# Hybrid decoder layer on one core: attention's output weights in two parts, and the order of the head groups in the first token tile

## The chip, the cores and the metric

The kernel runs on one NeuronCore of a Trainium2 chip (trn2). The metric is the device time of one launch in microseconds (us). The kernel before took 1487.29 us, the median of three runs between 1485.58 and 1488.57 us.

## The reference

One decoder layer over 2048 tokens of width 1024, all in float32. The normed tokens go through one input projection whose columns belong to three groups of heads; each group gives 512 columns, the three are set side by side, and one output projection brings them back to width 1024.

```
proj = rms_norm(x, g_pre) @ w_in
y_rg = rg_lru(conv(rg_x)) * silu(rg_g)                    # group 0: recurrence
y_da = rms_norm(diff_attention(q, k, v)) * silu(da_g)     # group 1: causal differential attention
y_xa = mem_cross_attention(xa_q, km, vm) * silu(xa_g)     # group 2: 256 memory tokens
y = concatenate([y_rg, y_da, y_xa]) @ w_out               # w_out is 1536 x 1024
out = x + rms_norm(y, g_post)
```

## The kernel before, in words

**Numbers in two parts.** Every float32 operand of a large product is split into a high part (a cast on ACT, L237) and a low part (raw minus high, on POOL or DVE, L238; `split_weight`). A product is then three matmuls (`mm3`, L240 to L243): high by high, low by high, high by low. In the output projection the token side is the stationary operand, so the first two matmuls read the high part of the weights and the third the low part.

**Stages.** `project` (L800) runs twice, first for the tokens 0 to 1023, then for 1024 to 2047; each time it walks through 16 pairs of column blocks, and a pair has four units (two token chunks by two halves) of 24 matmuls each. A unit ends in an eviction; for the last pair of the second run, a query and key pair, that is `ev_qk` (L425 to L441), which writes a tile `qkhl` and stores it to DRAM a little later. Attention runs as generators beside the projection: `pump` puts their matmuls between those of the projection when the modelled time `now` says that they are due. The first half of the attention's list of jobs (all heads, tokens 0 to 1023) precedes the second half.

**The output projection** (from L937) goes through 16 token tiles of 128 rows. A tile has two halves of 512 output columns and three head groups; a half and group take four blocks of 128 rows of the weights, 12 matmuls, into one of two PSUM tiles (`psM`, which the projection's units used before). The weights of a group are four blocks of 128x1024 (512 KB), loaded into a raw tile `woraw` and split in two halves of 512 columns, the first half's low part on POOL, the second's on DVE (L919 to L924). The split tokens of a tile and group (`y_granule`, L904) come through a raw tile of 256 KB, `yraw`, and the low part is made on POOL. Group 0's weights and the first granule are loaded inside the last pair, in `last_pair` (L927), which is called ahead of its third unit; the rest follows after the projection. In the first tile (token tile 0) a group is used for both halves before the next group; from tile 1 on all groups of one half come first. When a group's second half is done, the next tile's granule of that group is loaded.

**Buffers.** Groups 0 and 2 have their weights in the large pool (`wout` in the profile). Group 1's are named `wo`: blocks 0 to 2 take the six slots of `pw`, which the input weights (`wp`) held before, and block 3 two slots of `p4`. `p4` has seven slots of 4 KB per partition, and `qkhl`, `woraw`, the granules `yg`, block 3 of `wo`, and in the tiles `res` and `xres` all share them.

**Order.** TensorE's order is the order of the code (manual schedule). The other engines' orders, SP's queue of DMA issues among them, are made ahead of time by a list scheduler: by priority, which falls in the order of the code (some evictions are raised), as far as a cost model thinks operands and slots are ready. All loads and stores here are issued from SP's queue in that order, and one that waits for a slot holds up those behind it.

Of the kernel before, what the change touches and what calls it, by code (L numbers as in the profile page):

```python
# [10 lines left out]
F32R = mybir.dt.float32r  # L11
# [4 lines left out]
D = 1024  # L16
# [41 lines left out]
def hybrid_layer(  # L58
# [19 lines left out]
    pw = ctx.enter_context(tc.tile_pool(name="pw", bufs=6))  # L78
    p4 = ctx.enter_context(tc.tile_pool(name="p4", bufs=7))
# [9 lines left out]
    def f4(name, shape=(128, 1024), dt=F32, pool=p4):  # L89
        return pool.tile(list(shape), dt, tag="f4", name=name)  # L90

    def f2(name, shape=(128, 516), dt=F32, pool=p2):
        return pool.tile(list(shape), dt, tag="f2", name=name)

    def bigt(name, shape, dt=F32R):
        return big.tile(list(shape), dt, tag="big", name=name)

    def ps_m(name, shape=(128, 512)):
        return psM.tile(list(shape), F32, tag="M", name=name)
# [115 lines left out]
    def pump():  # L215
        busy = True
        while busy:
            busy = False
            for st in list(streams):
                if st[0] <= now[0]:  # L220
                    d = next(st[1], None)
                    if d is None:
                        streams.remove(st)
                    else:
                        st[0] = now[0] + d
                    busy = True
# [9 lines left out]
    def split_weight(raw, hi, lo, eng=nc.gpsimd):  # L236
        nc.scalar.copy(hi, raw)  # L237
        eng.tensor_sub(lo, raw, asf(hi))  # L238

    def mm3(o, wh, wl, xh, xl, first, last):  # L240
        mm(o, wh, xh, first, False)
        mm(o, wl, xh, False, False)
        mm(o, wh, xl, False, last)  # L243

    def rsqrt_mean(r, ss, n, eng=nc.gpsimd):

        v = tiny.tile(list(r.shape), F32, tag="rsv", name="rsv")
        t = tiny.tile(list(r.shape), F32, tag="rst", name="rst")
        eng.tensor_scalar(v, ss, 1.0 / n, EPS, op0=ALU.mult, op1=ALU.add)
        nc.scalar.activation(r, v, AF.Ln)  # L250
        nc.scalar.activation(r, r, AF.Exp, scale=-0.5)
        eng.tensor_mul(t, r, r)
        eng.tensor_mul(t, t, v)
        eng.tensor_scalar(t, t, -0.5, 1.5, op0=ALU.mult, op1=ALU.add)
        eng.tensor_mul(r, r, t)
# [346 lines left out]
    normed = set()  # L602
# [299 lines left out]
    wout, grans = {}, {}  # L902

    def y_granule(tt, grp):  # L904
        g = f4("yg", (128, 2, 4, 128), F32R)
        raw = praw.tile([128, 512], F32, tag="raw", name="yraw")
        nc.sync.dma_start(raw, YD[grp][tt // 4][tt % 4])
        split_weight(raw, g[:, 0].rearrange("p a b -> p (a b)"), g[:, 1].rearrange("p a b -> p (a b)"))
        return g


    def load_wout(grp):

        if grp == 1:
            t = [[f4("wo", (128, D), F32R, pw if kb < 3 else p4) for kb in range(4)] for _ in range(2)]
        else:
            bt = [bigt("wout", (128, 4, D)) for _ in range(2)]
            t = [[b[:, kb, :] for kb in range(4)] for b in bt]
        for kb in range(4):  # L919
            raw = f4("woraw")  # L920
            nc.sync.dma_start(raw, w_out[4 * grp + kb])
            for j in range(2):
                cs = slice(j * 512, (j + 1) * 512)
                split_weight(raw[:, cs], t[0][kb][:, cs], t[1][kb][:, cs], nc.vector if j else nc.gpsimd)  # L924
        wout[grp] = t

    def last_pair():  # L927
        grans[0, 0] = y_granule(0, 0)
        load_wout(0)

    project((2, 3), 80, ORDER_B, {(0, 0): start_b, (15, 2): last_pair})


    def y_ready(tt, grp):
        return grp != 1 or all((h, tt // 2) in normed for h in range(4))

    state["kind"] = "out"  # L937
    grans[0, 2] = y_granule(0, 2)
    load_wout(2)
    if y_ready(0, 1):  # L940
        grans[0, 1] = y_granule(0, 1)
    load_wout(1)
    gp = [f2("gp", (128, 512)) for _ in range(2)]
    for j in range(2):
        nc.sync.dma_start(gp[j], g_post[j * 512:(j + 1) * 512].unsqueeze(0).to_broadcast([128, 512]))

    GRP = (0, 2, 1)

    def get_y(tt, grp):
        if (tt, grp) not in grans:  # L950
            drain(lambda: y_ready(tt, grp))
            grans[tt, grp] = y_granule(tt, grp)
        return grans[tt, grp]

    for tt in range(NT):
        res = f4("res")
        ss = tiny.tile([128, 2], F32, tag="oss", name="oss")
        os = [None, None]

        order = [(half, grp) for half in range(2) for grp in GRP] if tt else \  # L960
                [(half, grp) for grp in GRP for half in range(2)]
        for half, grp in order:
            cs = slice(half * 512, half * 512 + 512)
            g, wt = get_y(tt, grp), wout[grp]
            if os[half] is None:
                os[half] = ps_m("po")
            o = os[half]
            for kb in range(4):
                mm3(o, g[:, 0, kb, :], g[:, 1, kb, :], wt[0][kb][:, cs], wt[1][kb][:, cs],
                    grp == GRP[0] and kb == 0, grp == GRP[2] and kb == 3)  # L970
                pump()
            if half == 1:
                del grans[tt, grp]
                if tt + 1 < NT and y_ready(tt + 1, grp):
                    grans[tt + 1, grp] = y_granule(tt + 1, grp)
            if grp == GRP[2]:
                junk = f2("junk", (128, 512))
                nc.scalar.activation(junk, o, AF.Square, accum_out=ss[:, half:half + 1])
                nc.vector.tensor_mul(res[:, cs], o, gp[half])
        r = tiny.tile([128, 1], F32, tag="r3", name="r3")  # L980
        xt = f4("xres")
        nc.sync.dma_start(xt, x[tt * 128:(tt + 1) * 128, :])
        nc.vector.tensor_add(ss[:, 0:1], ss[:, 0:1], ss[:, 1:2])
        rsqrt_mean(r, ss[:, 0:1], D, nc.vector)
        for j in range(2):
            cs = slice(j * 512, (j + 1) * 512)
            nc.vector.scalar_tensor_tensor(res[:, cs], res[:, cs], r, xt[:, cs], op0=ALU.mult, op1=ALU.add)
            if tt == NT - 1:
                nc.sync.dma_start(out[tt * 128:(tt + 1) * 128, cs], res[:, cs])
        if tt < NT - 1:  # L990
            nc.sync.dma_start(out[tt * 128:(tt + 1) * 128, :], res)
# [58 lines left out]
```

## Time and profile before

| | us |
|---|---|
| runs of the kernel before, median (lowest, highest) | 1487.29 (1485.58, 1488.57) |
| the profiled execution | 1490.95 |
| its span in the trace | 1489.10 |
| its mean granted TensorE clock | 0.986 of full speed |

The profiled execution lies 3.66 us above the median, and 1.85 us of it lie outside the span. PE is the matmul engine, PEld its weight loads, DVE VectorE, ACT ScalarE, POOL GpSimd, SPq SyncE's queue of DMA issues. A row of a timeline gives the start, the time from the first start to the last end, engine, line, operation, the tiles and the count of like instructions that were merged; in brackets stands the idle time of the engine before it and what ended it. Matmuls overlap: one is busy for some 0.39 us, and with 512 columns at full clock the next starts 0.23 us after it.

### The profile page before, as it was taken

Reading aid. Unit: us, or ns where it says so; the run is one execution under the profiler, and the core shown is the slowest. Engines: PE = TensorE matmul, PEld = TensorE weight load, DVE = VectorE, ACT = ScalarE, POOL = GpSimd, SP = SyncE. Lnnn points to the kernel's source line nnn. Section 1 sums busy time; section 2 is a strip of 40 time slices with the busy share of each in tenths; the row PEclk is TensorE's granted clock in tenths of the full one; section 3 lists DMA queues with packets and bytes.
Section 4 is the critical chain, followed back from the end, with each engine's and each line's share of the span. In section 5 each row is a group of like instructions: output and inputs, shape, how many; then the busy total and the mean of one; then the engine's idle time right before and its main releaser. Section 6 shows DMA issues by size and latency. Waiting matters only on the chain.

```text
span 1489.1 us, 21951 instructions
## 1 busy us (share of the span) xinstructions
PE 1422.1 (95%) x7568; PEld 1208.6 (81%) x7568; DVE 918.4 (62%) x1862; ACT 811.5 (54%) x1972; POOL 563.8 (38%) x634
## 2 busy tenths in 40 slices
PE   5999999999998899899998999999999999999997
PEld 4789889888886678787786898888877888888886
DVE  6332565677545776757648576767778777777222
ACT  6343545666458674755556555666566545554221
POOL 2231433443446543535425343423346433334221
PEclk9999999999999899999999999999999999999999
DMA  6666666342322146244222543221375234322231
GB/s 218 162 214 219 177 172 206 99 132 82 106 68 64 50 128 187 72 151 123 84 68 71 163 141 128 68 85 40 116 237 174 86 133 151 103 96 76 99 123 70
DMA packets 138655, 184.05 MB, mean 124 GB/s; under 512 B 11440, under 2 KB 81200, under 8 KB 138544
## 3 DMA queue, kind: packets, MB, share of 16 engines
q1 hardware_dynamic: 138400, 182.64, 39.6%
q8 instruction: 59, 0.97, 0.3%
q14 instruction: 52, 0.43, 0.1%
q10 hardware_dynamic: 144, 0.01, 0.0%
HBM read 125.99 MB, written 56.62 MB: 123 GB/s over the span
## 4 chain that ended last, share of the span: by engine, by line
PE 74%; DVE 8%; ACT 6%; POOL 5%; issue 4%; DMA 2%; SPq 0%; DVEq 0%; POOLq 0%; ACTq 0%
PE ip L197 35%; PE po L197 17%; PE s L197 7%; PE o L197 6%; PE pt L201 4%; DVE e L719 2%; PE xas L197 2%; PE kv L197 1%; POOL e L718 1%; PE xao L197 1%; POOL wp L238 1%; DMA wraw<-in_w_in_dram 1%; PE rgo L197 1%; DVE xc L553 1%; ACT e L695 1%
## 5 line engine op out<-in xcount | busy, mean ns | idle before, releaser
L197 PE MATMUL ip<-hnT,wp 128*128 128x512 f32 x2688 | 676.8, 397 | 4.9 <-DVE rgg L563 4.9
L197 PEld LDWEIGHTS ip<-hnT,wp 128*128 128x128 f32 x2688 | 499.0, 190 | 105.8 <-DVE rgg L563 6.1
L695 ACT ACTIVATE e<-s,nm 128x512 f32<-128x512 f32 (+3 forms) x320 | 200.0, 625 | 233.4 <-DVE nm L693 216.3
L238 POOL TENSOR_TENSOR wp<-wraw,wp 128x512 fp32r<-128x512 f32 x133 | 182.2, 1380 | 201.8 <-ACT wp L237 192.8
L693 DVE TENSOR_REDUCE nm<-s 128x1 f32<-128x512 f32 (+3 forms) x320 | 193.2, 605 | 32.4 <-PE s L197 27.7
L197 PE MATMUL po<-wout,yg 128*128 128x512 f32 x768 | 193.5, 393 | 4.2 <-POOL wout L238 1.9
L718 POOL TENSOR_SCALAR e<-e,f 128x512 f32<-128x512 f32 (+3 forms) x160 | 120.3, 767 | 171.1 <-DVE f L714 93.5
L197 PE MATMUL s<-kv,q 128*128 128x512 f32 (+3 forms) x640 | 182.8, 367 | 1.0 <-ACT e L695 0.9
L197 PEld LDWEIGHTS po<-wout,yg 128*128 128x128 f32 x768 | 141.3, 188 | 34.3 <-POOL wout L238 3.3
L719 DVE SCALAR_TENSOR_TENSOR e<-e,f 128x512 f32<-128x512 f32 (+3 forms) x160 | 142.7, 919 | 28.5 <-POOL e L718 28.3
L197 PE MATMUL o<-pthl,kv 128*128 128x256 f32 (+1 forms) x864 | 136.3, 293 | 2.0 <-DVE pthl L760 2.0
L760 DVE TENSOR_TENSOR pthl<-pt,pthl 128x512 fp32r<-128x512 f32 (+1 forms) x144 | 94.6, 657 | 70.4 <-ACT pthl L759 70.0
L197 PEld LDWEIGHTS s<-kv,q 128*128 128x128 f32 x640 | 114.6, 189 | 21.8 <-ACT e L695 1.3
L197 PEld LDWEIGHTS o<-pthl,kv 128*128 128x128 f32 x864 | 116.1, 192 | 5.6 <-DVE pthl L760 2.8
L238 POOL TENSOR_TENSOR yg<-yraw,yg 128x512 fp32r<-128x512 f32 x48 | 64.2, 1341 | 133.1 <-ACT yg L237 122.0
L237 ACT CAST wp<-wraw 128x512 fp32r<-128x512 f32 x144 | 88.2, 618 | 43.9 <-PE ip L197 22.1
L759 ACT CAST pthl<-pt 128x512 fp32r<-128x512 f32 (+1 forms) x144 | 80.8, 561 | 53.3 <-PE pt L201 52.7
L197 PE MATMUL ip<-wp,hnT 128*128 128x256 f32 x768 | 99.4, 284 | 0.0
L197 PE MATMUL po<-wo,yg 128*128 128x512 f32 x384 | 97.3, 392 | 0.0
L197 PEld LDWEIGHTS ip<-wp,hnT 128*128 128x128 f32 x768 | 96.2, 192 | 1.2
L201 PE MATMUL pt<-ident,e 128*128 128x128 f32 x544 | 84.4, 276 | 5.6 <-DVE pthl L760 5.6
L201 PEld LDWEIGHTS pt<-ident,e 128*128 128x128 f32 x544 | 67.9, 142 | 20.8 <-DVE pthl L760 6.0
(183 smaller groups left out, 1731.2 us busy)
## 6 DMA issues: line engine op xcount, KB each, us to landing
wraw<-in_w_in_dram SPq DMA_DIRECT2D x128, 256.0 KB, 2.7
q<-QD SPq DMA_DIRECT2D x128, 128.0 KB, 3.3
kv<-KD SPq DMA_DIRECT2D x24, 512.0 KB, 5.7
kv<-VD SPq DMA_DIRECT2D x24, 512.0 KB, 5.0
yraw<-YD SPq DMA_DIRECT2D x48, 256.0 KB, 2.7
QD<-qkhl SPq DMA_DIRECT2D x32, 256.0 KB, 3.3
KD<-qkhl SPq DMA_DIRECT2D x32, 256.0 KB, 3.7
VD<-vhl SPq DMA_DIRECT2D x32, 256.0 KB, 2.8
```

Of the source, the lines that this page charges most:

```text
L197: nc.tensor.matmul(o, w, xx, start=start, stop=stop)
L201: nc.tensor.transpose(o, i, ident)
L237: nc.scalar.copy(hi, raw)
L238: eng.tensor_sub(lo, raw, asf(hi))
L553: nc.vector.scalar_tensor_tensor(xc[:, 0:CH], xr[:, k:k + CH], vec2[:, cw + k:cw + k + 1], xc[:, 0:CH], op0=ALU.mult, op1=ALU.add)
L693: nc.vector.tensor_reduce(out=nm[:, c, kc:kc + 1], in_=s[:, 0:w], op=ALU.max, axis=AX.X, negate=True)
L695: nc.scalar.activation(e[kc, c][:, 0:w], s[:, 0:w], AF.Exp, bias=nm[:, c, kc:kc + 1], accum_out=l[:, c, kc:kc + 1])
L718: nc.gpsimd.tensor_scalar(e2, e2, f[:, 1, kc:kc + 1], 1.0, op0=ALU.mult, op1=ALU.mult)
L719: nc.vector.scalar_tensor_tensor(e1, e1, f[:, 0, kc:kc + 1], e2, op0=ALU.mult, op1=ALU.add)
L759: nc.scalar.copy(hi[:, 0:n], t[:, 0:n])
L760: nc.vector.tensor_sub(lo[:, 0:n], t[:, 0:n], asf(hi[:, 0:n]))
```

## The change

`load_wout` takes a list of blocks, so that a group can be loaded in two calls. `last_pair` now also loads the first tile's granule of group 1 (where its results are ready) and blocks 0 and 1 of group 1's weights; blocks 2 and 3 are loaded right after the projection, ahead of group 2's granule and weights. Block 1 instead of block 3 takes the two slots of `p4`. The first token tile uses the groups in the order 0, 1, 2; all later tiles keep 0, 2, 1.

```
-    def load_wout(grp):
-        if grp == 1:
-            t = [[f4("wo", (128, D), F32R, pw if kb < 3 else p4) for kb in range(4)] for _ in range(2)]
-        else:
-            bt = [bigt("wout", (128, 4, D)) for _ in range(2)]
-            t = [[b[:, kb, :] for kb in range(4)] for b in bt]
-        for kb in range(4):
+    def load_wout(grp, kbs=range(4)):
+        t = wout.setdefault(grp, [[None] * 4 for _ in range(2)])
+        if grp != 1:
+            for i in range(2):
+                b = bigt("wout", (128, 4, D))
+                t[i][:] = [b[:, kb, :] for kb in range(4)]
+        for kb in kbs:
+            if grp == 1:
+                for i in range(2):
+                    t[i][kb] = f4("wo", (128, D), F32R, p4 if kb == 1 else pw)
             raw = f4("woraw")
             nc.sync.dma_start(raw, w_out[4 * grp + kb])
             for j in range(2):
                 cs = slice(j * 512, (j + 1) * 512)
                 split_weight(raw[:, cs], t[0][kb][:, cs], t[1][kb][:, cs], nc.vector if j else nc.gpsimd)
-        wout[grp] = t
+
+    def y_ready(tt, grp):
+        return grp != 1 or all((h, tt // 2) in normed for h in range(4))
 
     def last_pair():
         grans[0, 0] = y_granule(0, 0)
         load_wout(0)
+        if y_ready(0, 1):
+            grans[0, 1] = y_granule(0, 1)
+        load_wout(1, (0, 1))
 
     state["kind"] = "out"
+    load_wout(1, (2, 3))
     grans[0, 2] = y_granule(0, 2)
     load_wout(2)
-    if y_ready(0, 1):
-        grans[0, 1] = y_granule(0, 1)
-    load_wout(1)
...
-    GRP = (0, 2, 1)
...
+        GRP = (0, 2, 1) if tt else (0, 1, 2)
         order = [(half, grp) for half in range(2) for grp in GRP] if tt else \
                 [(half, grp) for grp in GRP for half in range(2)]
```

## Rows read from the trace of the kernel before

**Rows 1.** The page's part 1, engines: busy us (share), instructions.

```profile
PE 1422.1 (95%) x7568; PEld 1208.6 (81%) x7568; DVE 918.4 (62%) x1862; ACT 811.5 (54%) x1972; POOL 563.8 (38%) x634
```

**Rows 2.** Busy time by stretch: stretch, length, engines' busy us (count), PE clock, DMA share, GB/s.

```profile
1100.00:1150.00 50.00, 45.07 (x214) 36.30 (x214) 40.69 (x77) 30.65 (x77) 31.04 (x29) 0.97 0.66 221
```

**Rows 3.** Groups of PE from 1141 to 1482 us: busy, mean ns, idle before.

```profile
L197 PE MATMUL po<-wout,yg 128*128 128x512 f32 x720 | 179.3, 392 | 1.1 <-DVE res L979 1.1
```

**Rows 4.** PE's timeline, first token tile and the start of the second.

```profile
1109.73 1.55 PE L197 MATMUL po<-wout,yg 128*128 128x512 f32 x6
...
1112.03 1.55 PE L197 MATMUL po<-wout,yg 128*128 128x512 f32 x6
1114.80 0.73 PE L197 MATMUL po<-wout,yg 128*128 128x512 f32 x2 [1.22 <-ACT wout L237]
1116.16 0.60 PE L197 MATMUL po<-wout,yg 128*128 128x512 f32 x1 [0.63 <-POOL wout L238]
...
1120.62 0.65 PE L197 MATMUL po<-wout,yg 128*128 128x512 f32 x2
1121.89 0.98 PE L197 MATMUL po<-wout,yg 128*128 128x512 f32 x3 [0.62 <-POOL wout L238]
1123.57 0.50 PE L197 MATMUL po<-wout,yg 128*128 128x512 f32 x1 [0.70 <-POOL wout L238]
...
1130.39 0.85 PE L197 MATMUL po<-wo,yg 128*128 128x512 f32 x3
...
1136.01 1.58 PE L197 MATMUL po<-wo,yg 128*128 128x512 f32 x6
...
1141.64 2.34 PE L197 MATMUL po<-wout,yg 128*128 128x512 f32 x9 [1.05 <-DVE res L979]
```

**Rows 5.** Busy time in the four microseconds after that stall; the clock stands eighth.

```profile
1116.00:1117.00 1.00, 0.84 (x3) 0.73 (x4) 0.65 (x1) 0.31 (x1) 1.00 (x2) 0.71 0.69 274
1117.00:1118.00 1.00, 1.00 (x7) 0.90 (x5) 0.53 (x2) 0.00 (x0) 1.00 (x2) 0.50 0.45 74
1118.00:1119.00 1.00, 1.00 (x7) 1.00 (x6) 0.42 (x2) 0.71 (x2) 1.00 (x1) 0.50 0.75 283
1119.00:1120.00 1.00, 1.00 (x5) 0.89 (x5) 0.60 (x1) 1.00 (x4) 0.03 (x1) 0.59 0.99 356
```

**Rows 6.** SP's timeline of DMA issues: the loads of weights behind the last pair.

```profile
1106.54 1.86 SPq L921 DMA_DIRECT2D woraw<-in_w_out_dram x3
1112.08 4.98 SPq L921 DMA_DIRECT2D woraw<-in_w_out_dram x2
```

**Rows 7.** SP's waits from 1087 to 1141.7 us: total, times, longest.

```profile
SPq L440 <- ACT qkhl L428: 6.7, 1, 6.7
SPq L921 <- DMA QD<-qkhl: 3.6, 1, 3.6
```

**Rows 8.** Busy time in the last pair's last ten microseconds.

```profile
1096.00:1100.00 4.00, 4.00 (x24) 3.47 (x23) 3.96 (x7) 3.59 (x8) 3.32 (x3) 1.00 0.49 187
1100.00:1105.80 5.80, 5.80 (x31) 4.87 (x31) 4.45 (x12) 1.99 (x7) 3.72 (x6) 1.00 0.72 186
```

**Rows 9.** The tile woraw: time from issue to landing.

```profile
DMA to landing us min/median/max: 3.5/5.6/8.8
```

**Rows 10.** The tile wo: ns min/median/max of each split instruction.

```profile
L237 ACT CAST wo<-woraw x8: 607/620/626, 1124.0 to 1132.9; 128x512 fp32r<-128x512 f32 x8
L238 POOL TENSOR_TENSOR wo<-woraw,wo x4: 1297/1455/1699, 1124.7 to 1134.4; 128x512 fp32r<-128x512 f32 x4
L238 DVE TENSOR_TENSOR wo<-woraw,wo x4: 681/687/812, 1126.4 to 1136.0; 128x512 fp32r<-128x512 f32 x4
```

**Rows 11.** The tile wout: the same subtraction on DVE.

```profile
L238 DVE TENSOR_TENSOR wout<-woraw,wout x8: 678/1300/1356, 1095.6 to 1124.2; 128x512 fp32r<-128x512 f32 x8
```

**Rows 12.** POOL's timeline: the third granule of tile 1.

```profile
1141.44 1.29 POOL L238 TENSOR_TENSOR yg<-yraw,yg 128x512 fp32r<-128x512 f32 x1
```

**Rows 13.** ACT's timeline: the last pair's last eviction.

```profile
1107.83 0.57 ACT L431 CAST qkhl<-ip 128x512 fp32r<-128x512 f32 x1
```

More of the change, by code (lines that the diff above doesn't have):

```diff
@@ L929, in last_pair @@
         load_wout(0)
+        if y_ready(0, 1):
+            grans[0, 1] = y_granule(0, 1)
+        load_wout(1, (0, 1))
     project((2, 3), 80, ORDER_B, {(0, 0): start_b, (15, 2): last_pair})
-    def y_ready(tt, grp):
-        return grp != 1 or all((h, tt // 2) in normed for h in range(4))
     state["kind"] = "out"
+    load_wout(1, (2, 3))
     grans[0, 2] = y_granule(0, 2)
     load_wout(2)
-    if y_ready(0, 1):
-        grans[0, 1] = y_granule(0, 1)
-    load_wout(1)
     gp = [f2("gp", (128, 512)) for _ in range(2)]
```

## The prediction

> **What bounds the kernel now.** I read the page's engine shares first: PE is busy 95% of the span, so time is saved only where PE stands still or runs slowly [rows 1]. The stretches by time come next: from 1100 to 1150 us PE is busy 45.07 of 50 us, the loosest place near the change [rows 2]. Behind it there is nothing to win: from 1141 to 1482 us the output projection's matmuls wait 1.1 us in all [rows 3], so what the first token tile gains or loses arrives whole at the end of the kernel.
>
> PE's own timeline then shows where the idle time lies [rows 4]. Group 0 of tile 0 runs without a gap until about 1113.6. Group 2 is next, and its matmuls stand still four times, each time for its weights `wout`: 1.22 us for a cast, then 0.63, 0.62 and 0.70 us for POOL's low parts, 3.17 us in all. Group 1, the third, starts at 1130.39 and no longer waits for weights. One more wait, 1.05 us at 1141.64, is for DVE to free a PSUM tile. The last view is the clock: in the four microseconds behind the first gap it stands at 0.71, 0.50, 0.50 and 0.59 of full speed, so for a while PE has its lower level, 1.2 instead of 2.4 GHz, right after it was idle [rows 5]. The lost parts add up to 0.29 + 0.50 + 0.50 + 0.41 = 1.70 us. Late weights therefore cost 3.17 + 1.70 = 4.87 us.
>
> Why they are late is in SP's queue: three blocks of group 2 leave at 1106.54, the fourth and the next one only at 1112.08 [rows 6], after a wait of 3.6 us for the store of the last query tile `qkhl`, which held a slot of `p4` [rows 7]. So slots of `p4` already set the pace.
>
> **The change part by part.** *Number of instructions.* None is added or removed: the same 12 blocks and granules are loaded and split, the same matmuls run, in the same places between attention's matmuls, since the first tile has 24 matmuls per group in any order. Only the tiles they read differ.
>
> *Two blocks and one granule move into the last pair.* That is 2 x 512 KB and 256 KB of transfer, five casts on ACT (5 x 0.62 = 3.1 us), three low parts on POOL (two of 1.46, one of 1.29: 4.2 us) and two on DVE. DMA has room: it is 0.49 and 0.72 busy in the two stretches there. ACT has room too (1.99 of 5.80 us from 1100). POOL is busy 3.32 of 4.00 and then 3.72 of 5.80 us, DVE 3.96 of 4.00 and then 4.45 of 5.80 us, a total of 1.39 us free [rows 8]. A low part on DVE takes 0.68 us where it runs alone [rows 10], but its median for `wout` is 1.30 us [rows 11], so two cost 1.4 to 2.6 us. DVE then falls behind by 0 to 1.2 us; attention's three score tiles in PSUM cover that, and I take 0. If the cover is gone, up to 1.2 us appear on PE.
>
> What speaks against the change here is a rule of the Trainium skill, "SBUF — State Buffer", on the shared pair of ports: GpSimd and a DVE operation with two SBUF inputs exclude each other, whichever starts first holds the pair for its whole instruction. The 0.68 against 1.30 us agree with that. By it, the added POOL work of 4.2 us can hold DVE up as well; that is rival D below.
>
> *Two blocks and group 2 stay behind it.* Without idle time and at full clock, the needs of tile 0 move up. By the rows, the second group reaches its third block at 1120.62 - 1.22 - 0.63 - 1.70 = 1117.1, its fourth at about 1118.0 to 1118.7; the third group starts at 1130.39 - 4.87 = 1125.5 and reaches its fourth block at 1136.01 - 4.87 = 1131.1 [rows 4]. Blocks 2 and 3 of group 1 stand in SP's queue where blocks 0 and 1 of group 2 stood. But `p4` is tighter: block 1 of group 1 (two slots) and the granule of group 1 are held from the last pair on, and with group 0's granule and the two `qkhl` tiles that is six of seven. So I let block 2 leave at 1106.54 and block 3 only with the freed slot, at 1112.08 [rows 6]. One turn of a slot is a landing of 3.5 us at best, 5.6 at the median [rows 9], two casts of 0.62 and a low part of 1.46 on POOL [rows 10]: 6.2 to 8.3 us. I take 7.0, nearer the short end, because 1 MB has left this stretch. Block 3 is ready at 1119.1, against 1118.0 to 1118.7: 0.8 us of wait (0 with 6.2 us, 2.3 with 8.3). Group 2's fourth block, third in that slot, is ready at 1112.08 + 3 x 7.0 = 1133.1 if two slots turn, against 1131.1 + 0.8 = 1131.9: 1.2 us late (0 with 6.2, 3.6 with 8.3); if the last `qkhl` store frees a third slot, it isn't late at all. I take 0.5. What remains is 1.3 us, with ends of 0 and 5.9.
>
> *Queues.* A waiting weight load holds up the key store, attention's query loads and tile 1's granules behind it on SP, as the 4.98 us at 1112.08 do now. Six blocks instead of eight stand there now, so these should leave no later; I take 0.
>
> *Tile 1's granules.* They are now asked for in the order 0, 1, 2 but used as 0, 2, 1. The third finishes on POOL at 1141.44 + 1.29 = 1142.7 [rows 12]. In the new order tile 1 wants it after 12 matmuls and some attention, about 3.6 us after its start, which moves from 1141.64 to about 1138.1: at 1141.7. Had POOL's order stayed, that would be 1.0 us late; POOL has lost three low parts ahead of it, so I take 0 and keep 1.0.
>
> *Sum.* -4.87 + 1.3 = -3.6 us on the profiled execution's 1490.95. That one lies 3.66 us above the median, and the difference counts from the median: 1487.29 - 3.6 = **1483.7 us**. About 0.2%, 3 us, is what a measurement of this kernel can tell from no change, so the forecast lies just beyond it.
>
> **The rivals.** *A, part of it comes back:* the turns take nearer 8 us, some 3.4 us of wait remain in groups 1 and 2, and the time is 1487.29 - 4.87 + 3.4 = 1485.8. For it: the longest landing of 8.8 us [rows 9]. Against: these were in the fullest stretch.
>
> *B, the loads don't leave earlier:* SP stands 6.7 us in the last pair, waiting for the third unit's eviction (L440) [rows 7]. If the two blocks are queued behind that, they leave with the others near 1106, and nothing changes: 1487.3. Against: they come before that store in the code, and group 0's raw tiles become free about then.
>
> *C, slower, a slot for the last eviction:* the last unit's `qkhl` needs a slot of `p4` at 1107.83 [rows 13], and its PSUM tile is wanted again by the second half of group 0 at 1109.73 [rows 4]. If the scheduler gives that slot to a weight block, the eviction waits until 1112.08, plus 0.57 for the cast and 0.68 for the low part: 1113.3, so PE stands 3.6 us, and the clock can drop once more (1.7 us). The next slot is then group 0's granule's, free at 1113.6 + 3.6 = 1117.2, so that block 3 is ready at 1124.2 against 1118 + 5.3 = 1123.3, and group 2's last at 1117.2 + 3 x 7.0 = 1138.2 against 1131.1 + 5.3 + 0.9 = 1137.3: 1.8 us more; with turns of 8.3 us it is 5.8. The change is then -4.87 + 5.3 + 1.8 = +2.2 up to +6.2 us; the middle is +4.2, 1491.5 us. It decides as soon as that cast starts later than about 1108.5. For it: six of seven slots are held. Against: evictions have a raised priority, and the low parts of the moved blocks have freed their raw tiles by then.
>
> *D, DVE becomes the bound in the last pair:* two low parts of 1.30 us and 4.2 us of POOL time that hold it up, less the 1.39 us free, would be 5.4 us at worst; if half of that passes attention's cover, 2.7 us, the time is 1483.7 + 2.7 = 1486.4. Against: most of DVE's work there reads scores from PSUM.
>
> **How the numbers follow.** Forecast 0.45, A 0.18, B 0.11, D 0.07, C 0.19. The forecast is faster by over 0.2%; A, B, D and a tenth of C (0.02) are within: 0.38; slower by over 0.2% is the rest of C, 0.17. The range begins at 1481.5: all 4.87 us gone and the 1.05 us of rows 4 as well give 1481.4. It ends at 1489.8, which holds A, B, D and the mild form of C, and leaves out its harder half. The forecast's own range is 1482.0 to 1484.3.
>
> **What would show it.** Right: in the new trace SP issues two `woraw` loads before the last unit ends, PE has under 1.5 us of idle time on `wo` and `wout` in tile 0, the clock stays at full speed there, and tile 1 starts 3 to 4 us earlier measured from the last `ip` matmul. Wrong in part: two low parts of `wo` on DVE before 1105 with PE idle on `s`, or an idle PE ahead of the second weight granule `yg` of tile 1. The forecast falls if the last `qkhl` cast is late with PE idle at group 0's second half, or if the weights of group 2 are now what tile 0 waits for.

## The result, and the profile after

The change made the kernel slower: 1494.81 us median (1493.01 to 1495.87) against 1486.43 us for the kernel before on the same chip, a ratio of 1.0053 with a 95% interval of 1.0036 to 1.0070. The forecast was 1483.7 us, and the result lies above the whole range. The profiled execution has a span of 1493.7 us at a mean granted clock of 0.983.

Upstream of the last pair, where neither the change nor most experiments touch anything, the profiles differ by several us, since the clock falls to its lower level there in three to seven places, with 8.5 to 17.1 us lost. So the stretch of the change is measured by itself: **L** is the time from the end of the last `ip` matmul to tile 1's first `po` matmul. Before, the last `ip` matmuls end at 1104.41 + 1.55 = 1105.96 and tile 1 starts at 1141.64 [rows 4], so L is 35.68 us. In PE's timeline after:

```profile
1101.48 1.55 PE L197 MATMUL ip<-hnT,wp 128*128 128x512 f32 x6
1106.43 1.65 PE L197 MATMUL po<-wout,yg 128*128 128x512 f32 x3 [3.40 <-DVE qkhl L429]
...
1119.50 0.74 PE L197 MATMUL po<-wo,yg 128*128 128x512 f32 x2 [0.52 <-ACT wo L237]
1121.01 0.97 PE L197 MATMUL po<-wo,yg 128*128 128x512 f32 x3 [0.77 <-POOL wo L238]
1122.77 0.50 PE L197 MATMUL po<-wo,yg 128*128 128x512 f32 x1 [0.79 <-POOL wo L238]
...
1135.82 0.73 PE L197 MATMUL po<-wout,yg 128*128 128x512 f32 x2 [1.65 <-ACT wout L237]
1137.17 0.80 PE L197 MATMUL po<-wout,yg 128*128 128x512 f32 x1 [0.62 <-POOL wout L238]
...
1146.03 1.32 PE L197 MATMUL po<-wout,yg 128*128 128x512 f32 x5
```

The last `ip` matmuls end at 1103.03 and tile 1 starts at 1146.03: L is 43.00 us, **7.3 us more**, which agrees with the whole cost of the change (the medians differ by 8.4 us, with 5.4 to 10.4 by the interval). Against rows 4 there is a new wait of 3.40 us ahead of group 0, which belongs to no weight but to the third unit's eviction (L429). Group 1, now second, waits 0.52 + 0.77 + 0.79 = 2.08 us and group 2 1.65 + 0.62 = 2.27 us, where group 2 as second waited 3.17 us before. The 1.05 us for `res` are gone. The clock falls three times instead of once; the stretches by time (stretch, length, busy time of PE, PEld, DVE, ACT, POOL, then clock, DMA share, GB/s), with rows 5 as their counterpart:

```profile
1106.40:1109.80 3.40, 3.37 (x8) 2.70 (x9) 2.81 (x6) 0.11 (x1) 2.24 (x3) 0.53 0.63 125
1123.40:1126.80 3.40, 3.40 (x14) 3.07 (x14) 1.91 (x6) 0.59 (x1) 1.92 (x3) 0.52 0.79 242
1136.90:1143.80 6.90, 6.63 (x19) 5.48 (x20) 3.27 (x5) 4.26 (x11) 5.71 (x7) 0.51 0.51 172
```

That loses 3.40 x 0.47 + 3.40 x 0.48 + 6.90 x 0.49 = 6.6 us. Idle time and lost clock are now 7.75 + 6.6 = 14.4 us, against 3.17 + 1.05 + 1.70 and 0.70 on attention's `pthl`, 6.6 us, before: 7.7 us more, which covers the 7.3. Of these, 3.40 + 1.6 = 5.0 us go with the new wait. The other idle time of PE is even less than before (4.35 against 4.92 us), so the rest is lost clock. From tile 1 on nothing differs: PE is busy 339.92 of 341 us after (from 1146) and 339.88 before (from 1141).

**Why the eviction is late.** The third unit's matmuls end about 1096.0 (its fourth unit is the last 24 `ip` matmuls: 6 from 1101.48, 12 from 1098.27 and the last 6 of 9 from 1095.27). ACT's timeline after:

```profile
1100.14 0.47 ACT L695 ACTIVATE e<-s,nm 128x256 f32<-128x256 f32 x1
1100.51 0.19 ACT L695 ACTIVATION_READ_ACCUMULATOR e<-s,nm 128x1 f32 x1
1100.60 1.13 ACT L237 CAST wo<-woraw 128x512 fp32r<-128x512 f32 x2
1101.63 0.21 ACT L709 ACTIVATE f<-f 128x6 f32<-128x6 f32 x1
1101.74 1.13 ACT L237 CAST wo<-woraw 128x512 fp32r<-128x512 f32 x2
1102.77 0.59 ACT L428 ACTIVATE qkhl<-ip 128x512 fp32r<-128x512 f32 x1
```

and DVE's, which makes the eviction's second part:

```profile
1101.77 1.36 DVE L238 TENSOR_TENSOR wo<-woraw,wo 128x512 fp32r<-128x512 f32 x1 [1.95 <-ACT wo L237]
1103.05 1.22 DVE L710 TENSOR_TENSOR l<-l,f 128x6 f32<-128x6 f32 x1
1104.19 0.68 DVE L693 TENSOR_REDUCE nm<-s 128x1 f32<-128x512 f32 x1
1104.80 0.14 DVE L711 TENSOR_REDUCE r<-l 128x2 f32<-128x6 f32 x1
1104.97 0.17 DVE L712 RECIPROCAL r<-r 128x2 f32<-128x2 f32 x1
1105.08 0.69 DVE L238 TENSOR_TENSOR wo<-woraw,wo 128x512 fp32r<-128x512 f32 x1
1105.69 0.68 DVE L429 SCALAR_TENSOR_TENSOR qkhl<-ip,qkhl 128x512 fp32r<-128x512 f32 x1
```

In ACT's timeline of the kernel before, the same cast stands right at the end of its matmuls:

```profile
1099.09 0.60 ACT L428 ACTIVATE qkhl<-ip 128x512 fp32r<-128x512 f32 x1
```

Now it starts 6.8 us after them. It stands in ACT's order behind the four casts of the moved blocks, and its second part behind their two low parts on DVE; until it is done at 1106.37, group 0's first half has no PSUM tile. This is the order that the scheduler made.

Before, the cast waited for PE alone. Now, by the semaphores in the trace, it waits for the two stores of the second unit's `qkhl`, so it has that tile's slot. On the chip those were over in time: they left at 1087.94 and 1088.58 and landed 6.2 to 6.3 us later. Of the two waits, the one that ACT's sequencer takes passed at 1100.0 within 17 ns, as the instructions of line L428 show (ns min/median/max, first and last start), and the cast follows the last of the four without idle time:

```profile
L428 ACTq EVENT_SEMAPHORE  x1: 17/17/17, 1100.0 to 1100.0; - x1
```

So it isn't the slot that was late, but the place in the order that the scheduler gave the eviction.

POOL's added work makes the wait on DVE longer. DVE has no idle time from 1101.77 to the end of the eviction, and its first two instructions there stand beside POOL's low parts of the moved blocks:

```profile
1101.29 2.96 POOL L238 TENSOR_TENSOR wo<-woraw,wo 128x512 fp32r<-128x512 f32 x2
```

DVE's low part takes 1.36 us there and 0.69 us at 1105.08, where POOL is idle. L710, on six columns, takes 1.22 us and ends with POOL's work; with POOL idle it takes 0.16 us. That is 0.67 + 1.06 = 1.7 us, an estimate from these rows of what POOL adds to the 3.40 us of wait; no run has the change without it.

**Why the groups behind it wait.** SP's timeline after, the loads of blocks and the stores of the evictions:

```profile
1094.15 0.91 SPq L924 DMA_DIRECT2D woraw<-in_w_out_dram  x2
...
1108.40 0.64 SPq L440 DMA_DIRECT2D QD<-qkhl  x1
...
1110.88 5.25 SPq L924 DMA_DIRECT2D woraw<-in_w_out_dram  x2
...
1121.66 2.00 SPq L924 DMA_DIRECT2D woraw<-in_w_out_dram  x2
...
1130.66 1.39 SPq L924 DMA_DIRECT2D woraw<-in_w_out_dram  x2
```

A merged row gives the start of its first load only. The two moved blocks leave early, as intended. The last transfer of the third unit's store, ahead of the other loads on this queue, leaves at 1108.40; before it left at 1104.62, and with 2.93 us less upstream it is 6.7 us late. Block 2 leaves 7.85 us after the last `ip` matmul (0.58 before for the block in that place [rows 6]). Block 3 leaves only at 1115.79. SP's waits from 1108 to 1142 us (total, times, longest) say why:

```profile
SPq L924 <- PE po L197: 4.4, 1, 4.4
```

PE's last matmul of group 0 ends that wait, so block 3 takes the slot of group 0's granule. From there on two slots turn: the one of block 2 after 10.8 and 9.0 us (1110.88, 1121.66, 1130.66), the one of block 3 after 7.5 us (1123.33). The last block leaves at 1131.12, behind the others, in the slot of the fourth unit's `qkhl`. In the turn of 10.8 us block 2 had landed at 1115.40, but its casts stand behind attention's work on ACT until 1118.83, and its low part on DVE ends at 1121.58:

```profile
1118.83 1.14 ACT L237 CAST wo<-woraw 128x512 fp32r<-128x512 f32 x2
1120.90 2.36 DVE L238 TENSOR_TENSOR wo<-woraw,wo 128x512 fp32r<-128x512 f32 x2
```

### The profile page after: what moved, and what is told of

It reads as the page before. It is cut to its first block, busy times and chain, and to the rows that moved or that the text cites. A ratio compares the mean times of both kernels' runs of the same rounds, so it can differ in the third digit from the quotient of the medians.

```text
span 1493.7 us, 21954 instructions
## 1 busy us (share of the span) xinstructions
PE 1425.6 (95%) x7568; PEld 1211.4 (81%) x7568; DVE 914.1 (61%) x1862; ACT 811.7 (54%) x1972; POOL 562.1 (38%) x634
## 5 line engine op out<-in xcount | busy, mean ns | idle before, releaser
L197 PEld LDWEIGHTS po<-wout,yg 128*128 128x128 f32 x768 | 143.3, 191 | 35.7 <-DVE qkhl L429 3.8
L719 DVE SCALAR_TENSOR_TENSOR e<-e,f 128x512 f32<-128x512 f32 (+3 forms) x160 | 141.1, 909 | 27.7 <-POOL e L718 27.4
L197 PEld LDWEIGHTS po<-wo,yg 128*128 128x128 f32 x384 | 71.2, 189 | 17.5 <-POOL wo L238 2.4
```

The lines of the kernel that those rows point to most:

```text
L197: nc.tensor.matmul(o, w, xx, start=start, stop=stop)
L719: nc.vector.scalar_tensor_tensor(e1, e1, f[:, 0, kc:kc + 1], e2, op0=ALU.mult, op1=ALU.add)
```

## The experiments

Three theories stood against each other. **Slots:** block 1's two tiles and group 1's granule hold three of `p4`'s seven slots from the last pair on. **Work:** the moved blocks' casts and low parts delay the evictions on ACT and DVE. **Order:** tile 0's new order of groups costs something itself. Each run, with L, PE's idle time in tile 0 on the last evictions and on weights, and the clock lost in L (L times what its mean granted clock lacks to full speed), all but the ratio from one profile each:

| run | ratio (95%) | L, us | wait on eviction | waits on weights | lost clock |
|---|---|---|---|---|---|
| before | 1 | 35.7 | none | 3.2 | 1.7 |
| the change | 1.0053 (1.0036 to 1.0070) | 43.0 | 3.40, third | 4.4 | 6.8 |
| e1 order alone | 1.0005 (0.9991 to 1.0019) | 36.4 | none | 5.1 | 1.7 |
| e2 moves alone | 1.0049 (1.0029 to 1.0068) | 46.6 | 3.39, third | 7.8 | 6.8 |
| e3 block 0 and granule | 1.0024 (1.0009 to 1.0040) | 39.9 | 0.76, fourth | 4.7 | 5.1 |
| e6 block 0 | 1.0036 (1.0019 to 1.0053) | 40.0 | 0.51, fourth | 5.6 | 5.1 |
| e7 change, p4 8 | 1.0022 (1.0011 to 1.0033) | 37.3 | 3.41, third | 2.1 | 1.7 |
| e8 before, p4 8 | 1.0005 (0.9992 to 1.0017) | 35.2 | none | 3.6 | 0 |
| e5 change, tile claimed first | 1.0067 (1.0042 to 1.0091) | 47.7 | 3.64, fourth | 7.8 | 10.2 |
| e9 before, extra split work | 1.0038 (1.0023 to 1.0053) | 40.7 | 3.95, fourth | 2.4 | 3.4 |
| e10 before, half raw tiles | 0.9990 (0.9977 to 1.0003) | 35.4 | none | 2.8 | 1.7 |
| e11 change, half raw tiles | 0.9988 (0.9976 to 1.0001) | 33.9 | 0.51, fourth | 2.4 | 0 |
| e12 order alone, half raw tiles | 1.0003 (0.9992 to 1.0015) | 37.5 | none | 5.7 | 3.4 |
| e13 change, split late | 1.0034 (1.0017 to 1.0051) | 40.4 | 0.15, fourth | 5.4 | 6.8 |

**The order, and the moves.** e1 has the new order of groups with nothing in the last pair:

```
     def last_pair():
         ...
-        if y_ready(0, 1):
-            grans[0, 1] = y_granule(0, 1)
-        load_wout(1, (0, 1))
...
-    load_wout(1, (2, 3))
+    if y_ready(0, 1):
+        grans[0, 1] = y_granule(0, 1)
+    load_wout(1)
```

(block 3 in `p4` again). Expected:

> Order of tile 0 alone (0, 1, 2, group 1's granule and all four weight blocks after the projection, ahead of group 2's); nothing is moved into the last pair. Theory 1 (slots: the seven slots of p4 are short, since block 1's two tiles and group 1's granule are held from the last pair on): PE's wait of 3.4 us for the third unit's eviction (DVE L429) is gone; the second group waits for weights about as group 2 did before (3.2 us idle and 1.7 us of clock), the third 0 to 3 us, since block 3 now takes its two slots earlier: 1486 to 1490 us. Theory 2 (work: the added splits overload ACT and DVE in the last pair, whatever the slots): all of the loss goes, 1486 to 1487 us. Theory 3 (the order 0, 1, 2 itself is what costs): the loss stays, 1493 us or more.

e2 has the moves and the old order, group 2's loads ahead of blocks 2 and 3:

```
-        GRP = (0, 2, 1) if tt else (0, 1, 2)
+        GRP = (0, 2, 1)
```

Expected:

> The moves alone: granule and blocks 0 and 1 of group 1 in the last pair, then group 2's granule and weights, then blocks 2 and 3; tile 0 keeps the order 0, 2, 1. Theories 1 and 2: PE waits 3.4 us for DVE L429 as in the changed kernel, the clock falls after it, and group 2 then waits for its weights, 3 us or more: 1492 to 1498 us. Theory 3: no loss, 1485 to 1488 us.

Measured: e1 is as fast as before, e2 loses as much as the change in time (and 3.6 us more in L), with the same wait of 3.39 us on L429. The theory that the order makes the loss falls, and the loss comes with the moves.

**Parts of the moves.** e3 moves only block 0 (`load_wout(1, (0,))`) and the granule, with block 3 in `p4`; e6 only block 0. Expected:

> As the changed kernel, but only block 0 of group 1 (two slots of pw) and the granule go into the last pair; block 1 comes after the projection and block 3 takes the slots of p4, as before. Theory 1: the third unit's eviction stands ahead of the splits again, so the 3.4 us wait for L429 is gone; the second group waits for weights 0 to 3 us, group 2 somewhat: 1484 to 1489 us. Theory 2: half of the added work is still there, so 1 to 2 us of the wait for L429 remain: 1488 to 1491 us.

> As e3_block0_only, but group 1's granule too is loaded after the projection, so that the last pair takes nothing of p4 but the raw tile in passing; order 0, 1, 2. Theory 1: the last pair runs as before, and behind it one block less is to be loaded with the slots of before: tile 1 starts 34 to 37 us after the last ip matmul, 1484 to 1488 us. Theory 2: one block's splits are still added to the last pair, so a wait of 1 to 2 us for an eviction appears: 37 to 39 us.

Measured: L 39.9 and 40.0. The wait on the third unit's eviction is gone in both, and some 3 of the 7.3 us with it; what is left are waits for weights and 3.4 us more of lost clock than before. No theory had expected that: e3's 1492.0 us lie above both of its ranges, and so does e6's L, though its granule no longer holds a slot. SP's timeline of e6 shows as slow a pace:

```profile
1107.59 3.64 SPq L924 DMA_DIRECT2D woraw<-in_w_out_dram  x3
...
1112.82 0.59 SPq L438 DMA_DIRECT2D KD<-qkhl  x1
1122.11 2.90 SPq L924 DMA_DIRECT2D woraw<-in_w_out_dram  x2
1125.06 0.59 SPq L438 DMA_DIRECT2D KD<-qkhl  x1
...
1131.55 2.14 SPq L924 DMA_DIRECT2D woraw<-in_w_out_dram  x2
```

Half of the fourth unit's key store stands on SP behind loads that wait for slots, and holds its own slot until it leaves at 1125.06. So one held slot less need not bring one turning slot more; that the queue is what stands in the way is read from this order and was not tested.

**The number of slots.** e4 takes one slot from the kernel before (`p4` 6). Expected:

> The kernel before with six slots in p4 instead of seven, nothing moved. Theory 1: weights of groups 2 and 1 come later than before, several us of further waits in tile 0 and clock drops after them: 1489 to 1495 us, with no change of order. Theories 2 and 3: no loss in tile 0, 1486 to 1488 us.

Measured: 1.0262 (1.0240 to 1.0284), but L only 36.8. Tile 1 starts 378.8 us before the end, where all other runs have 347.0 to 348.4, so that some 31 of the 39 us lost lie in the later tiles of the output projection. The run says nothing on the loss in tile 0. e7 and e8 add one slot:

```
-    p4 = ctx.enter_context(tc.tile_pool(name="p4", bufs=7))
+    p4 = ctx.enter_context(tc.tile_pool(name="p4", bufs=8))
-    p2 = ctx.enter_context(tc.tile_pool(name="p2", bufs=9))
+    p2 = ctx.enter_context(tc.tile_pool(name="p2", bufs=7))
```

Expected:

> The changed kernel with eight slots in p4 and seven instead of nine in p2, to be held against e8. Theory 1: the second ring (the loads of weights behind the projection) gains a slot, so the waits for weights shrink from 5 us of idle time to under 3; the eviction's wait shrinks only if the scheduler gives it the new slot. Tile 1 starts 2 to 5 us nearer to e8 than the changed kernel to the one before (7.3 us). Theory 2: the distance to e8 stays at 7 us.

> The kernel before with eight slots in p4 and seven in p2. Theory 1: group 2's blocks come a little earlier, tile 1 starts 33 to 35.7 us after the last ip matmul. Theory 2: 35.7 us. Both: what fewer tiles of p2 cost attention shows in the whole time alike in e7 and e8.

Measured: the change's distance in L shrinks from 7.3 to 37.3 - 35.2 = 2.1 us. The third group waits no more and the clock falls once. But the wait on the eviction stays as it was, in PE's timeline of e7

```profile
1105.54 0.96 PE L197 MATMUL po<-wout,yg 128*128 128x512 f32 x3 [3.41 <-DVE qkhl L429]
```

and ACT's, with the same four casts ahead of the eviction's:

```profile
1099.70 1.13 ACT L237 CAST wo<-woraw 128x512 fp32r<-128x512 f32 x2
1100.73 0.21 ACT L709 ACTIVATE f<-f 128x6 f32<-128x6 f32 x1
1100.84 1.13 ACT L237 CAST wo<-woraw 128x512 fp32r<-128x512 f32 x2
1101.88 0.59 ACT L428 ACTIVATE qkhl<-ip 128x512 fp32r<-128x512 f32 x1
```

So one slot more shortens the later waits of the changed kernel (4.4 to 2.1 us for weights), and the eviction still stands behind the four casts, although in e7 it waits for no store (its only wait is for ACT itself).

**A slot for the eviction.** e5 claims the third unit's `qkhl` at the head of `last_pair`, ahead of the moved tiles:

```
+        state["held"] = t = f4("qkhl", (128, 2, CH), F32R)
+        nc.vector.memset(asf(t)[:, 0, 0:1], 0.0)
```

Expected:

> The changed kernel, but the tile for the third unit's eviction is claimed ahead of the granules and weights of the last pair (a one-column memset on DVE, which the eviction overwrites). All splits stay in the last pair. The measure is the time from the end of the last ip matmul to the start of tile 1: 35.7 us before, 43.0 us in the changed kernel. Theory 1 (slots of p4): the eviction stands ahead of the splits, PE's 3.4 us wait for the third unit's DVE eviction and the 1.7 us of clock behind it go, while the later waits for weights stay or grow a little: 37 to 40 us, 1487 to 1492 us in all. Theory 2 (the added splits overload ACT and DVE): 2 us or more of that wait stay, 41 us or more.

Measured: missed, L is 47.7. The first wait is gone, but the fourth unit's eviction (L432, here L434) takes its place, and the groups wait more. PE's timeline of e5:

```profile
1113.14 2.93 PE L197 MATMUL po<-wout,yg 128*128 128x512 f32 x6 [3.64 <-DVE qkhl L434]
```

**The work alone.** e9 is the kernel before with two of group 0's blocks split twice, so that the last pair has the added split work and no added tile:

```
+                for _ in range(2 if grp == 0 and kb > 1 else 1):
-                split_weight(raw[:, cs], t[0][kb][:, cs], t[1][kb][:, cs], nc.vector if j else nc.gpsimd)
+                    split_weight(raw[:, cs], t[0][kb][:, cs], t[1][kb][:, cs], nc.vector if j else nc.gpsimd)
```

Expected:

> The kernel before, with group 0's blocks 2 and 3 split twice in the last pair (the same values written again): four casts on ACT, two low parts on POOL and two on DVE more, as two moved blocks bring, but no slot of p4 is held for their results. Theory 2 (the added work overloads ACT and DVE): PE waits 2 us or more for the third unit's DVE eviction, tile 1 starts 39 us or more after the last ip matmul (35.7 before, 43.0 in the changed kernel), 1490 us or more. Theory 1 (slots): no such wait, 35.5 to 37 us (the raw tiles are held a little longer), 1486 to 1489 us.

Measured: L 40.7, and PE waits 3.95 us at group 0's second half. DVE's timeline of e9:

```profile
1104.35 3.46 DVE L719 SCALAR_TENSOR_TENSOR e<-e,f 128x512 f32<-128x512 f32 x3 [0.23 <-POOL e L718]
1107.73 0.68 DVE L432 TENSOR_TENSOR qkhl<-ip,qkhl 128x512 fp32r<-128x512 f32 x1
```

The low parts push attention's small steps back: the last of them, L714, ends 3.0 us after the last `ip` matmul, and before it ended 1.5 us ahead of it. Three long ones (L719), which stood ahead of the fourth unit's eviction before as well, come that much later, and the eviction with them. Before, that ended at 1108.43 + 0.69 = 1109.12, 0.6 us ahead of its use at 1109.73 [rows 4]: there was no more slack than that. Work alone can cost 4 us, so neither theory is enough.

**Raw tiles out of p4.** e10, e11 and e12 take the odd blocks of groups 1 and 2 through `praw`, in two tiles of 256 KB each; the moves, the order and the split work stay:

```
-            raw = f4("woraw")
-            nc.sync.dma_start(raw, w_out[4 * grp + kb])
+            if not (grp and kb % 2):
+                raw = f4("woraw")
+                nc.sync.dma_start(raw, w_out[4 * grp + kb])
             for j in range(2):
                 cs = slice(j * 512, (j + 1) * 512)
+                if grp and kb % 2:
+                    rj = praw.tile([128, 512], F32, tag="raw", name="woraw")
+                    nc.sync.dma_start(rj, w_out[4 * grp + kb][:, cs])
+                else:
+                    rj = raw[:, cs]
```

Expected:

> The kernel before; only the odd blocks of groups 1 and 2 come as two halves of 256 KB through the three small raw tiles that the granules use, instead of through p4. Nothing else changes. Theory 1: the loads of weights turn in p4, so with half of them out of it they arrive earlier: of 3.2 us idle and 1.7 us of clock in the second group over half goes, tile 1 starts 31.5 to 34 us after the last ip matmul, 1483 to 1486 us. Rival (transfer rate or the splits themselves are the limit): 35 to 36 us, no difference.

> The changed kernel with the odd blocks of groups 1 and 2 through the small raw tiles, as in e10. Theory 1: the waits for weights in groups 1 and 2 (4.3 us idle, 5.1 us of clock) mostly go, and the third unit's eviction, which now stands behind one of the two moved blocks only, waits under 1.5 us: 32 to 37 us from the last ip matmul to tile 1, 1483 to 1488 us. Theory 2, or the order of groups as a cause: 40 us or more.

> As e1 (order 0, 1, 2 in tile 0, nothing moved into the last pair) with the odd blocks through the small raw tiles. Theory 1: as e10, 31.5 to 34.5 us from the last ip matmul to tile 1, 1483 to 1486 us. If the order costs something by itself, it is 1 us or more above e10.

Measured: the edit does nothing to the kernel before (L 35.4, as e10's rival had it and not the slots theory) and takes all of the loss from the change (33.9, as e11's slots theory had it). ACT's timeline of e11:

```profile
1094.66 1.13 ACT L237 CAST wo<-woraw 128x512 fp32r<-128x512 f32 x2
1095.69 0.60 ACT L428 ACTIVATE qkhl<-ip 128x512 fp32r<-128x512 f32 x1
...
1098.89 0.62 ACT L237 CAST wo<-woraw 128x512 fp32r<-128x512 f32 x1
...
1099.87 0.61 ACT L237 CAST wo<-woraw 128x512 fp32r<-128x512 f32 x1
```

With one moved raw tile fewer in `p4`, the eviction stands ahead of two of the four casts, 4.4 us before the end of the last `ip` matmul (1100.09), and the moves now cost nothing. e12, the order without the moves, is no better than e1 and has an L 2.1 us above e10's, which its expectation would call a price of the order. As 1.7 of the 2.1 us are one more fall of the clock, and e1's L is 0.8 us above before's, the runs don't settle whether the order costs a little.

**Held tiles without the work.** e13 loads the moved blocks as early as the change, but splits them behind the projection:

```
-        load_wout(1, (0, 1))
+        for kb in range(2):
+            held[1, kb] = raw = f4("woraw")
+            nc.sync.dma_start(raw, w_out[4 + kb])
...
-    load_wout(1, (2, 3))
+    load_wout(1)
```

Expected:

> The kernel after, with one part undone: blocks 0 and 1 of group 1's weights are loaded in the last pair as in the change, but their casts and low parts stand behind the projection; until then their raw tiles keep two slots of p4 (as block 1's two tiles did). So the slots are held, and the added split work is not in the last pair. L is the time from the last ip matmul to tile 1's first po matmul: 35.7 us before, 43.0 after. Slots alone: the third unit's eviction still waits for its slot, PE stands 2 to 4 us at group 0's first half on qkhl, L is 42 to 48, ratio 1.004 to 1.007. Split work alone: that wait is gone, the six other blocks still turn in two slots, L is 38 to 40, ratio 1.002 to 1.003. Both needed together: no wait there and L at most 37.

Measured: close to what was expected of the work theory (L 40.4). The wait on the third unit's eviction is gone though three slots are held: its cast starts at 1095.90, 5.4 us before the end of the last `ip` matmul. The other blocks still turn slowly (loads from 1107.98, 1116.78 and 1124.55 on, two each), and group 1 waits 2.25 + 0.55 us, group 2 1.92 + 0.63 us. So the first wait needs the split work in the last pair, in a place ahead of the eviction. The later waits come without it, but whether from the held slots or from the splits that now come later, e13 doesn't tell; e1, with nothing held in the last pair, waits 5.1 us for weights as well.

**A faster version?** e14 is e11 with `p4` 8 and `p2` 7, e15 with `praw` 5 (it has 3) and `p2` 7, e16 with `praw` 4 and `p2` 8; e17 is the kernel before with e16's pool sizes alone, e18 e16 once more beside it. Expected:

> The kernel after with the odd blocks of groups 1 and 2 through the pool praw in halves (as the run before with that edit, L 33.9 us, ratio 0.9988), and p4 8 slots, p2 7. Slots theory: 0.5 to 1 us less again, as the waits of 0.64 and 0.84 us on low parts of wo shrink; L 32.5 to 34, ratio 0.998 to 0.9995, if p2's two fewer slots cost nothing upstream (in the two runs with eight slots they cost 0 to 1 us). Work theory: the wait on DVE's eviction stays and nothing changes: L 33.5 to 34.5.

> The kernel after with the odd blocks of groups 1 and 2 through praw in halves, and praw 5 slots instead of 3, p2 7 instead of 9. Slots theory: the halves and the granules' raw tiles turn in three slots of praw, so with five the remaining waits for low parts of wo and wout (2.4 us in all with three) fall below 1.2 us: L 32 to 33.5, ratio 0.9975 to 0.999. If POOL's own speed sets those waits and not the slots: L 33.5 to 34.5, ratio 0.9985 to 1.0.

> As the run with five slots of praw, but four, and p2 8. Slots theory: between the runs with three and five, L 32.5 to 34, ratio 0.998 to 0.9995. If POOL's speed sets the waits: L 33.5 to 34.5, ratio 0.9985 to 1.0.

> The kernel before, with praw 4 slots instead of 3 and p2 8 instead of 9, and nothing else. The version with the change, half raw tiles and these pool sizes came out at a ratio of 0.9978, but the stretch around tile 0 (L 35.4 us) was no shorter than before's 35.7. If the pool sizes bring the gain upstream of the last pair, this kernel has it too: ratio 0.997 to 0.999, L 35 to 36. If they do nothing by themselves and the gain belongs to tile 0: ratio 0.9995 to 1.001.

> The kernel of e16 once more, beside e17 on one chip, as one interval of five rounds doesn't settle 0.2%. If e16's gain is real: ratio 0.997 to 0.999, L 34.5 to 35.5. If it was the scatter of the half-clock stretches upstream: ratio 0.999 to 1.001.

| run | ratio (95%) | L, us |
|---|---|---|
| e14 | 1.0001 (0.9991 to 1.0010) | 34.0 |
| e15 | 0.9988 (0.9978 to 0.9999) | 34.5 |
| e16 | 0.9978 (0.9966 to 0.9990) | 35.4 |
| e17, before with e16's pools | 0.9983 (0.9972 to 0.9995) | 34.9 |
| e18, e16 again | 0.9977 (0.9966 to 0.9987) | 34.8 |

e14 and e15 have the L of their rivals (33.5 to 34.5), and e16's lies above both of its ranges. e16 and e18 beat the kernel before by 3.3 and 2.8 us (1484.39 against 1487.68 and 1484.47 against 1487.25 us). But e17, which has nothing of the change, has nearly all of it. So the gain belongs to the pool sizes (`praw` 4 with `p2` 8, which no run parts) and not to the moved blocks. L is only 0.8 us shorter than before's in e17, so most of it lies upstream, where no single wait of PE accounts for it; its cause stays open. Group 1 waits 0.63, 0.85 and 0.62 us in e16, as in e11: more slots of `praw` don't shorten these.

## Why the prediction was wrong, point by point

**Where the time stood, right.** Behind tile 1's start nothing moved, and the 1.05 us for `res` went, as the lower end of the range had it.

**Why group 2's weights were late, misread.** "So slots of `p4` already set the pace" doesn't hold for the first gap: the first block left at 1106.54 without a wait for a slot, landed 7.6 us later, and PE's 1.22 + 0.63 us of idle time and the clock fall of 1.70 us came right behind it. ACT's timeline of the kernel before:

```profile
1114.13 1.14 ACT L237 CAST wout<-woraw 128x512 fp32r<-128x512 f32 x2 [0.34 <-DMA woraw<-in_w_out_dram]
```

One slot more (e8) left PE's waits for weights at 3.6 us, and half of the raw tiles out of `p4` (e10) at 2.8, against 3.2. The row at 1112.08 [rows 6] was misread too: its second load left only at 1116.73.

**The loads leave early, right.** The two blocks left at 1094.15, 8.9 us before the end of the last `ip` matmul; rival B falls.

**The first failed step: "attention's three score tiles in PSUM cover that, and I take 0".** The step counted free time per engine ("ACT has room too") and asked only how long the added work takes. What counts is what stands behind it in the engine's order: there it was an eviction, whose PSUM tile group 0 needs, and score tiles don't cover that. ACT and DVE were even idle in between (1.95 us on DVE ahead of the first low part). Price: 3.40 us and a clock fall of 1.6. e11 and e13 show it by their order, e9 that DVE's queue has the same weakness at the next eviction, with 0.6 us of slack. What the runs don't settle is what made the scheduler place the eviction so: one raw tile fewer in `p4` moves it ahead (e11), one slot more doesn't (e7). In the change and in e2 the eviction has a slot for which it waits for two stores. In e3, e6, e11 and e13, where it comes in time, it waits for no store. But in e7 it waits for no store either and still stands behind the casts.

**The second: the turn of a slot, "7.0, nearer the short end".** It measured 7.5 us in one slot, but 10.8 and 9.0 in the other, beyond the 8.3 that was the long end, since block 2's casts started 3.4 us after its landing, behind attention's work on ACT, and its low part 0.9 us after the casts. The starts were wrong too. The "queues" step, "these should leave no later", took the first one from rows 6: block 2 left 7.3 us later, behind the late eviction's stores. And block 3 did not get the slot of the `qkhl` store "at 1112.08", 6.1 us after the last `ip` matmul, but that of group 0's granule, 12.8 us after it. The residual taken as 0.8 + 0.5 us was 2.08 + 2.27 us, with two clock falls of 1.6 and 3.4 us that the sum did not have. e7's extra slot takes 5.7 us of L away, 5.1 of them clock. As such falls vary from profile to profile (last section), the idle time is the firmer part of this price.

**Tile 1's granules, right.** No matmul of tile 1 waits for `yg`.

**The rivals.** C was the right kind: an eviction that comes late because the moved blocks take what it needs. But it looked at the fourth unit's, at group 0's second half, and took a slot that is late on the chip for the cause, where it was the order. That its price at that place, 3.6 + 1.7 us, is what the third unit's cost (3.40 + 1.6) is luck. Its next link was right: block 3 waited for the slot of group 0's granule. Its top of +6.2 us lay below the 7.3 in L, as its later waits were worked out with turns of at most 8.3 us. It had 0.19. D, with 0.07, looked for the wait on `s`, and PE has none there anywhere in tile 0; but its mechanism, POOL's added work holding DVE up, is in the eviction's wait, with up to 1.7 of the 3.40 us by the estimate above. The trace agrees with the shared ports of the Trainium skill ("SBUF — State Buffer", "SBUF: two separate sides"): DVE's low parts took 1.36 us beside POOL's and 0.69 without. No run isolates what that cost.

**The gain itself was small.** With the loss removed, e11 against e10, which differ by the change alone, stand at L 33.9 and 35.4, and their times at 0.9988 and 0.9990 of before. The 4.87 us that were to be won shrank to 1.5 us even there, since group 1 as second group still waits 2.1 us for its casts and low parts; and as the clock falls once in e10 and never in e11 (1.7 us), that too may be chance.

## What to carry to other kernels

Before work is moved into a busy stretch, look at what stands behind it in each engine's order, above all evictions that a matmul soon needs: free time on the engine says nothing of that. Where loads, stores and results share one pool and one issue queue, a load can wait for a slot, for a store ahead of it in the queue, or behind other work on the engines that free its slot; count the turns with the measured time from load to the last reader. Here, taking half of the raw tiles out of the shared pool took the loss away, but no gain of the move was left to see. And when a variant with other pool sizes wins, run the pool sizes alone.

## What the hardware showed

Nearly the same short gaps brought the clock down in one run and not in another. In e11 group 1 waits 0.64, 0.84 and 0.62 us between 1112.5 and 1115.8, in e18 0.63, 0.85 and 0.62 us between 1113.2 and 1116.5. The stretches by time of e11 (the clock stands ahead of the last two numbers)

```profile
1112.40:1119.20 6.80, 4.69 (x24) 3.49 (x24) 5.40 (x12) 3.44 (x8) 4.46 (x5) 1.00 0.60 187
```

and of e18:

```profile
1116.00:1122.20 6.20, 5.67 (x18) 4.86 (x19) 3.13 (x8) 2.50 (x7) 3.60 (x4) 0.50 0.76 231
```

e11 keeps 2.4 GHz throughout; e18 runs at 1.2 GHz for these 6.2 us and loses some 3.1. A gap of PE so has a price that varies by some 3 us from profile to profile, and differences in L below that are not to be read as an effect of the edit.

POOL held DVE up even in the smallest instructions. In the trace after, L710 on four to eight columns never takes more than 0.17 us where no POOL instruction overlaps it (33 times). In the 11 cases where POOL has more than 0.1 us of work left at its start, it ends within 0.03 us of the end of POOL's instruction and takes 0.22 to 1.22 us.
